# A SwiGLU up projection moved from weights stationary to tokens stationary with its output transposed, and weights split in pieces of 2048 columns

## The chip, the cores and the metric

The kernel runs on one core of a Trainium2 chip. The metric is the time of one execution in microseconds of the device (us), as the median of several runs. The engines that matter are TensorE (PE), which multiplies; VectorE (DVE) and ScalarE (ACT), which do element-wise work; GpSimd (POOL), which does small powers; and SyncE (SP), whose queue starts the transfers from memory.

## The reference

An encoder trunk of two layers (`DEPTH` = 2) in fp32, on 256 tokens of width 1024. Each layer is a half-step FFN, a mixing step of three branches, and another half-step FFN. The change is in the FFNs, and in how weights are made ready in all stages. `D_FF` is 2816. Cut to what matters:

```python
def swiglu(h, w_up, w_down):
    a, b = jnp.split(h @ w_up, 2, axis=-1)
    return (jax.nn.silu(a) * b) @ w_down
...
    for l in range(DEPTH):
        h = rms_norm(x, ffn1_pre_g[l])
        x = x + 0.5 * rms_norm(swiglu(h, ffn1_w_up[l], ffn1_w_down[l]), ffn1_post_g[l])
        h = rms_norm(x, mix_pre_g[l])
        u_pool, q_da, k_da, v_da, q_ca = jnp.split(h @ w_in[l], IN_SPLITS, axis=-1)
        ...
        x = x + rms_norm(merged @ w_out[l], mix_post_g[l])
        h = rms_norm(x, ffn2_pre_g[l])
        x = x + 0.5 * rms_norm(swiglu(h, ffn2_w_up[l], ffn2_w_down[l]), ffn2_post_g[l])
```

Between the two FFNs of a layer (the left-out lines) stand a pooling branch, a differential attention with two softmaxes per head, and a cross attention into 256 normed memory tokens; three gates weigh them.

## The kernel before

**Split weights and products.** Every weight arrives in units of 128 partitions x 2048 columns of fp32 (1 MB), each by one DMA on SP's queue (`load_unit`, L96-102). `next_unit` (L104-120) splits a unit in two tensors of the type fp32r: ACT casts a high part `wh` (L115), DVE subtracts it from the raw unit to get a low part `wl` (L116). The first five units of a stage (`FINE`) are split in four pieces of 512 columns, the others in two of 1024: ACT casts the first piece, DVE subtracts it while ACT casts the second. The raw units have 3 buffers, `wh` and `wl` 5 each. The activations are split in the same way (`split`, L148-150; ACT L149, DVE L150). A product is three matmuls: high x high, high x low, low x high.

**The FFN** (`ffn`, L266 on). The hidden columns go in 11 pairs p of 256 columns (2 x 128 of each half of `w_up`). The tokens are two chunks c of 128. Two forms of the up projection stand in the code:

- p = 0 and 1 use `up(p, c, ws)` (L295-312), called for each token chunk. The 128 tokens (`xhl`, the split and transposed input) are stationary, and 512 weight columns move: 256 for the Silu and 256 for the factor, 8 blocks of 128 rows, 24 matmuls into one PSUM bank `ma` (`form_b2` L232, `mm3`, its matmul is L207). Then ACT takes the Silu of one half (L300), DVE multiplies by the other (L302). The result has tokens on partitions, where `down` needs hidden columns there, so two PE transposes follow (L307, into a bank `mb`) and a split (L149, L150) into `hid[p]`. These are put off: `turn` is put on a list and `flush` issues it behind the matmuls of the next `up` or `up2`, or in the last part of the FFN.
- p = 2 to 10 use `up2(p, u)` (L314-327), called for each 128 hidden columns u. Here the weights are stationary and the tokens move (`form_a2`, L218-226): 512 moving columns (256 tokens high, 256 low, in four pieces of 128 of a tile) with the high weights, and 256 (two pieces) with the low ones, 16 matmuls for each of two banks, `ma` and `mb`. The result has hidden columns on partitions already. ACT copies out the low half of a bank (L323), DVE adds the high one (L324), for both banks; then the Silu (L325), the product (L326) and the split into `hid[p]`.

`down(p)` (L281) multiplies `hid[p]`, stationary, with a unit of `w_down`, 512 columns moving, 24 matmuls (L249). `down(p - 2)` follows `up` of p as long as p is at most 9; the last three p come in `tail` (L256), which goes through the token chunks one after the other, with `flush` between them. In the first FFN of a layer, `ahead()` prepares the memory tokens at p = 4, and PE transposes them (L182, 8 for each chunk, two banks `mb` each) at p = 6.

**The mix** (L406 on). Its input products are L207 as well. The steps of the attention on PE are placed by hand among the big products: `T_DA`, `T_PV`, `T_LN`, `T_CA`, `T_CAV` (L36-41) name after how many matmuls of a stage's count a group of small ones is issued. Before the transposes of `T_DA` (L449) lies a softmax: DVE finds the maximum (L421) and scales it (L423), ACT takes the exponentials (L429), DVE scales and combines (L565, L567, L569, L570). Before those of `T_CA` the scaling is L607 and L612. The copies out of the transposes are ACT's L451.

The order of the instructions within an engine is set by a scheduler when the program is built, and every engine then works strictly in that order: a short step on DVE waits for the long one that stands ahead of it.

Of the kernel before, what the change touches and what calls it, by code (L numbers as in the profile page):

```python
# [13 lines left out]
AF = mybir.ActivationFunctionType  # L14
ALU = mybir.AluOpType
AX = mybir.AxisListType

P = 128
D = 1024
KT = D // P  # L20
S = 256
DEPTH = 2
D_FF = 2816
# [23 lines left out]
def encoder_kernel(ctx, tc, x_d, mem_d, pos_d, w_d, gains_d, cols_d, lamv_d, poolw_d, cst_d, out_d):  # L47
    nc = tc.nc
# [15 lines left out]
    def acc_bank():  # L64
        return accp.tile([P, 512], F32, name="acc")

    def ma_bank():
        return mmp.tile([P, 512], F32, name="ma")

    def mb_bank():  # L70
        return mmp.tile([P, 512], F32, name="mb")

    def t2(shape=(P, 512), dt=F32):
        return s2.tile(list(shape), dt, name="s2")
# [19 lines left out]
    fine = [0]  # L94

    def load_unit(parts=1):  # L96
        raw = rawp.tile([P, 2048], F32, name="raw")
        n = 2048 // parts
        for i in range(parts):
            nc.sync.dma_start(out=raw[:, i * n:(i + 1) * n], in_=w_d[nxt[0]][:, i * n:(i + 1) * n])  # L100
        nxt[0] += 1
        raws.append(raw)

    def next_unit():  # L104
        parts = 4 if fine[0] > 0 else 2
        fine[0] -= 1
        if not raws:
            load_unit()
        raw = raws.pop(0)
        h = wts.tile([P, 2048], F32R, name="wh")  # L110
        l = wts.tile([P, 2048], F32R, name="wl")
        n = 2048 // parts
        for s in range(parts):
            cs = slice(s * n, (s + 1) * n)
            nc.scalar.copy(out=h[:, cs], in_=raw[:, cs])  # L115
            low = nc.vector.tensor_tensor(out=l[:, cs], in0=raw[:, cs], in1=h.bitcast(F32)[:, cs], op=ALU.subtract)  # L116
            if nxt[1] == 0:
                issue_after([low], first_xn[1])
        nxt[1] += 1
        return h, l  # L120
# [27 lines left out]
    def split(ps, h, l):  # L148
        nc.scalar.copy(out=h, in_=ps)  # L149
        nc.vector.tensor_tensor(out=l, in0=ps, in1=h.bitcast(F32), op=ALU.subtract)  # L150
# [60 lines left out]
    def kview(w):  # L211
        return w[0].rearrange("p (k m) -> p k m", k=KT), w[1].rearrange("p (k m) -> p k m", k=KT)
# [2 lines left out]
        wh, wl = kview(w)  # L215
        return mm3(out, [((wh[:, k, ms], wl[:, k, ms]), (xx[0][:, :, k, :], xx[1][:, :, k, :])) for k in range(KT)])

    def form_a2(out, w, ms, xx):  # L218
        wh, wl = kview(w)
        full, low = out, out[:, 0:S]  # L220
        for k in range(KT):
            todo = [(full, wh, xx[2][:, :, k, :]), (low, wl, xx[2][:, 0:2, k, :])]
            if k == KT - 1:
                todo.reverse()
            for o, ww, rhs in todo:
                nc.tensor.matmul(out=o, lhsT=ww[:, k, ms], rhs=rhs, start=(k == 0 and o is full), stop=(k == KT - 1 and o is full))  # L226

    def form_b(out, w, c, xx):
        wh, wl = kview(w)
        return mm3(out, [((xx[0][:, c, k, :], xx[1][:, c, k, :]), (wh[:, k, :], wl[:, k, :])) for k in range(KT)])  # L230
# [38 lines left out]
    def ffn(i, xx, late, g_post, finish, ahead):  # L269
        fine[0] = FINE  # L270
        hid = {}
        acc = [[None, None], [None, None]]

        def hid_pair(p):
            hid[p] = (hids.tile([P, 2, 2, P], F32R, name="hid"), hids.tile([P, 2, 2, P], F32R, name="hid"))
            return hid[p]

        def lhs_of(c, kk, k):
            return hid[kk][0][:, c, k, :], hid[kk][1][:, c, k, :]

        def down(p):  # L281
            w = next_unit()
            if p == 0:
                for c in range(2):
                    acc[c] = [acc_bank(), acc_bank()]
            for c in range(2):
                rows_chunk(c, acc[c], [(w, p)], lhs_of, 0, NPR - 1)

        pending = []

        def flush():
            while pending:
                pending.pop(0)()

        def up(p, c, ws):  # L295
            ps = ma_bank()
            now = form_b2(ps, ws[0], ws[1], c, xx)
            flush()
            sg = t2((P, 2, P))
            nc.scalar.activation(out=sg, in_=ps[:, 0:256].rearrange("p (u m) -> p u m", u=2), func=AF.Silu)  # L300
            hn = t2((P, 2, P))
            nc.vector.tensor_tensor(out=hn, in0=ps[:, 256:512].rearrange("p (u m) -> p u m", u=2), in1=sg, op=ALU.mult)  # L302

            def turn():
                tp = mb_bank()
                for u in range(2):
                    nc.tensor.transpose(out=tp[:, u * P:(u + 1) * P], in_=hn[:, u, :], identity=ident)  # L307
                tv = tp[:, 0:256].rearrange("p (u t) -> p u t", u=2)
                split(tv, hid[p][0][:, c], hid[p][1][:, c])

            pending.append(turn)
            return now

        def up2(p, u):  # L314
            w = next_unit()
            banks = [ma_bank(), mb_bank()]
            for i in range(2):
                form_a2(banks[i], w, slice(i * P, (i + 1) * P), xx)
            flush()
            t = t2()  # L320
            for i in range(2):
                half = t[:, i * S:(i + 1) * S]
                nc.scalar.copy(out=half, in_=banks[i][:, S:2 * S])  # L323
                nc.vector.tensor_tensor(out=half, in0=banks[i][:, 0:S], in1=half, op=ALU.add)  # L324
            nc.scalar.activation(out=t[:, 0:S], in_=t[:, 0:S], func=AF.Silu)  # L325
            nc.vector.tensor_tensor(out=t[:, 0:S], in0=t[:, 0:S], in1=t[:, S:2 * S], op=ALU.mult)  # L326
            split(t[:, 0:S].rearrange("p (c t) -> p c t", c=2), hid[p][0][:, :, u, :], hid[p][1][:, :, u, :])

        ws = [(next_unit(), next_unit()) for _ in range(2)]
        for p in range(2):  # L330
            hid_pair(p)
        done = []
        order = [(0, 0), (0, 1), (1, 0), (1, 1)] if i > 0 else [(0, 0), (1, 0), (0, 1), (1, 1)]
        for c, p in order:
            now = up(p, c, ws[p])
            done += now
            if len(done) == (48 if i > 0 else 24):
                issue_after(late, done[T_UP if i > 0 else T_FIRST])
        for p in range(2, NPR):
            hid_pair(p)  # L340
            for u in range(2):
                up2(p, u)
            if p - 2 <= NPR - 4:
                down(p - 2)
            if p == 4:
                turns = ahead()
            if p == 6:
                for t in turns:
                    t()
        todo = [(next_unit(), p) for p in range(NPR - 3, NPR)]  # L350
        return tail(acc, todo, lhs_of, 0, NPR - 1, g_post, True, finish, flush)
# [427 lines left out]
def _pack(a, np):  # L779
    L = DEPTH  # L780
    units = []

    def cols(w, idx):
        units.append(np.ascontiguousarray(w[:, idx].reshape(KT, P, 256).transpose(1, 0, 2)).reshape(P, 2048))

    def wide(w, idx):
        both = w[:, idx].reshape(2, 4, P, 512).transpose(0, 2, 1, 3)
        units.extend(np.ascontiguousarray(both[i]).reshape(P, 2048) for i in range(2))

    def rows(w, j):  # L790
        units.append(np.ascontiguousarray(w[256 * j:256 * (j + 1)].reshape(2, P, D).transpose(1, 0, 2)).reshape(P, 2048))

    def ffn(up, down):
        for p in range(NPR):
            if p < 2:
                wide(up, np.r_[256 * p:256 * p + 256, D_FF + 256 * p:D_FF + 256 * p + 256])
            else:
                for i in (2 * p, 2 * p + 1):
                    cols(up, np.r_[P * i:P * i + P, D_FF + P * i:D_FF + P * i + P])
            if 0 <= p - 2 <= NPR - 4:  # L800
                rows(down, p - 2)
        for p in range(NPR - 3, NPR):
            rows(down, p)

    for l in range(L):
        ffn(a["ffn1_w_up"][l], a["ffn1_w_down"][l])
        wi = a["w_in"][l]
        for s in (256, 768, 1280):
            wide(wi, slice(s, s + 512))
        for s in (0, 1792):  # L810
            cols(wi, slice(s, s + 256))
        for s in (0, 256):
            cols(a["w_mem_kv"][l], slice(s, s + 256))
        for i in range(6):
            wide(a["w_gate"][l], slice(512 * i, 512 * i + 512))
        br = np.concatenate([a["w_br_pool"][l], a["w_br_da"][l], a["w_br_ca"][l]], axis=0)
        for i in range(2):
            wide(br, slice(512 * i, 512 * i + 512))
        for j in range(4):
            rows(a["w_out"][l], j)  # L820
        ffn(a["ffn2_w_up"][l], a["ffn2_w_down"][l])
    return np.stack(units)
# [38 lines left out]
```

## Time and profile before

| what | value |
|---|---|
| time, median of 3 runs | 1155.15 us (1155.0 to 1155.38) |
| span of the profiled execution | 1154.1 us |
| PE busy | 1141.8 us, 5930 matmuls and transposes |
| DVE, ACT busy | 768.6 us, 634.1 us |
| memory read | 215.80 MB, 188 GB/s over the span |

The profiled execution is one of its own; its page shows the span, which lies about 1 us under the median time, for what lies around it. "Busy" of PE counts a matmul from its start to its modelled end, which lies in the next one's time, so the durations of matmuls (0.39 us) overlap and what one costs in a row is the distance from start to start. On ACT and DVE the durations also overlap a little. A row of the groups has the line, the engine, the operation, the tile written and the tiles read, the shapes, the count, the busy time and the mean of one, then the idle time of the engine ahead of the group and what ended it.

### The profile page before, as it was taken

How to read it: one execution, taken by the hardware profiler on the slowest of the kernel's cores; microseconds unless marked ns; L12 is line 12 of the kernel's file. 1: busy time of each engine (PE TensorE's matmuls, PEld its weight loads, DVE VectorE, ACT ScalarE, POOL GpSimd, SP SyncE). 2: the span in 40 equal slices, each digit the busy share in tenths (PEclk: the TensorE clock that was granted, in tenths of full speed). 3: DMA queues.
4: the chain of work that ended last, by engine and by line, in shares of the span. 5: the costliest groups of instructions: out<-in, count | busy, mean ns of one | idle time of the engine just before them, and what ended most of it. 6: DMA issues, size and time to landing. Idle time of an engine off the chain costs nothing.

```text
span 1154.1 us, 15241 instructions
## 1 busy us (share of the span) xinstructions
PE 1141.8 (99%) x5930; PEld 963.4 (83%) x5930; DVE 768.6 (67%) x1198; ACT 634.1 (55%) x1141; POOL 28.6 (2%) x39
## 2 busy tenths in 40 slices
PE   8999999999999999999999999999999999999997
PEld 5888888898888888888888888888978888888886
DVE  5768665665767876665586766675677678666653
ACT  5657554644665555555465655556455646555551
POOL 0000000000000100000000000010000001000000
PEclk8999999999999999999999999999999999999999
DMA  8865554564444575555456665535535544755530
GB/s 298 299 236 213 183 183 146 183 219 146 164 172 162 194 271 191 183 182 189 176 191 228 223 216 180 185 141 192 209 120 194 201 165 166 248 190 182 183 110 36
DMA packets 34055, 217.82 MB, mean 189 GB/s; under 512 B 4032, under 2 KB 4288, under 8 KB 9664
## 3 DMA queue, kind: packets, MB, share of 16 engines
q1 hardware_dynamic: 33984, 216.86, 53.0%
q8 instruction: 46, 0.75, 0.3%
q14 instruction: 25, 0.20, 0.0%
HBM read 215.80 MB, written 1.05 MB: 188 GB/s over the span
## 4 chain that ended last, share of the span: by engine, by line
PE 98%; DMA 1%; ACT 0%; SPq 0%; issue 0%; DVE 0%; DVEq 0%; POOLq 0%; ACTq 0%
PE ma L207 30%; PE acc L249 25%; PE mb L226 18%; PE ma L226 18%; PE mb L207 2%; PE mb L182 1%; PE acc L207 1%; PE acc L560 1%; DMA raw<-in_w 1%; PE mb L449 1%; PE acc L577 1%; PE acc L618 1%; PE acc L603 1%; PE mb L307 0%; PE mb L691 0%; PE mb L507 0%
## 5 line engine op out<-in xcount | busy, mean ns | idle before, releaser
L116 DVE TENSOR_TENSOR wl<-raw,wh 128x1024 fp32r<-128x1024 f32 (+1 forms) x444 | 460.2, 1077 | 140.2 <-ACT wh L115 125.9
L115 ACT CAST wh<-raw 128x1024 fp32r<-128x1024 f32 (+1 forms) x444 | 392.1, 935 | 169.8 <-issue 112.4
L207 PE MATMUL ma<-wh,xhl 128*128 128x512 f32 (+1 forms) x928 | 290.5, 390 | 1.9 <-ACT xhl L149 1.9
L249 PE MATMUL acc<-wh,hid 128*128 128x512 f32 x704 | 223.8, 390 | 0.0
L226 PE MATMUL ma<-xhl,wh 128*128 128x512 f32 x576 | 209.9, 399 | 0.0
L226 PE MATMUL mb<-xhl,wh 128*128 128x512 f32 x576 | 209.3, 398 | 0.0
L207 PEld LDWEIGHTS ma<-wh,xhl 128*128 128x128 f32 x928 | 172.8, 190 | 37.5 <-ACT xhl L149 2.2
L207 PE MATMUL ma<-wl,xhl 128*128 128x512 f32 (+1 forms) x464 | 180.2, 388 | 0.0
L249 PEld LDWEIGHTS acc<-wh,hid 128*128 128x128 f32 x704 | 132.2, 188 | 26.1
L226 PE MATMUL ma<-xhl,wl 128*128 128x256 f32 x576 | 150.1, 281 | 0.0
L226 PE MATMUL mb<-xhl,wl 128*128 128x256 f32 x576 | 150.1, 281 | 0.0
L249 PE MATMUL acc<-wl,hid 128*128 128x512 f32 x352 | 137.1, 389 | 0.0
L226 PEld LDWEIGHTS ma<-xhl,wh 128*128 128x128 f32 x576 | 108.2, 188 | 20.9
L226 PEld LDWEIGHTS mb<-xhl,wh 128*128 128x128 f32 x576 | 108.7, 189 | 19.2
L324 DVE TENSOR_TENSOR s<-mb,s 128x256 f32<-128x256 f32 x72 | 30.6, 425 | 130.2 <-ACT s L323 130.1
L226 PEld LDWEIGHTS mb<-xhl,wl 128*128 128x128 f32 x576 | 109.0, 189 | 6.6
L226 PEld LDWEIGHTS ma<-xhl,wl 128*128 128x128 f32 x576 | 108.8, 189 | 5.9
L207 PEld LDWEIGHTS ma<-wl,xhl 128*128 128x128 f32 x464 | 88.2, 190 | 17.3 <-issue 1.3
L249 PEld LDWEIGHTS acc<-wl,hid 128*128 128x128 f32 x352 | 66.2, 188 | 13.9
L325 ACT ACTIVATE s<-s 128x256 f32<-128x256 f32 x72 | 30.1, 418 | 69.5 <-DVE s L324 69.5
L323 ACT COPY s<-mb 128x256 f32<-128x256 f32 x72 | 26.8, 372 | 74.3 <-PE mb L226 74.3
L134 POOL TENSOR_TENSOR sm<-sm,mhalf 128x1 f32<-128x1 f32 (+1 forms) x32 | 27.9, 871 | 1119.8 <-DVE sm L143 855.2
(153 smaller groups left out, 991.3 us busy)
## 6 DMA issues: line engine op xcount, KB each, us to landing
raw<-in_w SPq DMA_DIRECT2D x190, 1024.0 KB, 4.9
gain<-in_gains SPq DMA_DIRECT2D x20, 512.0 KB, 5.2
raw<-in_w SPq DMA_DIRECT2D x4, 512.0 KB, 8.3
hid<-in_mem SPq DMA_DIRECT2D x8, 256.0 KB, 6.0
x<-in_x SPq DMA_DIRECT2D x4, 256.0 KB, 6.3
out<-x SPq DMA_DIRECT2D x4, 256.0 KB, 2.1
cst<-in_cst SPq DMA_DIRECT2D x1, 304.0 KB, 5.3
pw<-in_poolw SPq DMA_DIRECT2D x2, 128.0 KB, 4.0
```

The source lines that it names most:

```text
L115: nc.scalar.copy(out=h[:, cs], in_=raw[:, cs])
L116: low = nc.vector.tensor_tensor(out=l[:, cs], in0=raw[:, cs], in1=h.bitcast(F32)[:, cs], op=ALU.subtract)
L134: nc.gpsimd.tensor_tensor(out=r, in0=v, in1=mhalf[:, :n], op=ALU.pow)
L182: tps.append(nc.tensor.transpose(out=ps[:, k * P:(k + 1) * P], in_=xn[:, i * P:(i + 1) * P], identity=ident))
L207: done.append(nc.tensor.matmul(out=out, lhsT=lhsT, rhs=rhs, start=(i == 0), stop=(i == n - 1)))
L226: nc.tensor.matmul(out=o, lhsT=ww[:, k, ms], rhs=rhs, start=(k == 0 and o is full), stop=(k == KT - 1 and o is full))
L249: done.append(nc.tensor.matmul(out=banks[b], lhsT=a, rhs=ww[:, k, fs], start=(kk == first and k == 0 and i == 0), stop=(kk == last and k = ...
L323: nc.scalar.copy(out=half, in_=banks[i][:, S:2 * S])
L324: nc.vector.tensor_tensor(out=half, in0=banks[i][:, 0:S], in1=half, op=ALU.add)
L325: nc.scalar.activation(out=t[:, 0:S], in_=t[:, 0:S], func=AF.Silu)
L449: ins.append(nc.tensor.transpose(out=tp[:, i * P:(i + 1) * P], in_=a[:, hh, kt * P:(kt + 1) * P], identity=ident))
L560: nc.tensor.matmul(out=banks[m][:, hh * S:(hh + 1) * S], lhsT=qT[rs, c, 2 * hp + hh, :], rhs=kT[rs, :, 2 * hp + hh, :], start=True, stop=True)
```

## The change

All pairs p use the form of p = 0 and 1. The two units of a pair are now packed as p = 0 and 1 had them (512 wide: 256 columns of each half of `w_up`, 4 of the 8 row blocks in each unit), `up(p, c, w2)` is called for both chunks, and `form_a2` and `up2` go. The number and size of the units stay. Apart from the first five units of a stage, a unit is split whole: one cast of 2048 columns and one subtraction. In the new code, lines up to about L313 stand 10 lower (L307 becomes L297, L249 L239, L300 L290, L302 L292) and those behind 24 lower (L421 becomes L397, L423 L399, L449 L425, L570 L546, L612 L588).

```diff
     def next_unit():
-        parts = 4 if fine[0] > 0 else 2
+        parts = 4 if fine[0] > 0 else 1
         fine[0] -= 1
...
-    def form_a2(out, w, ms, xx):
-        wh, wl = kview(w)
-        full, low = out, out[:, 0:S]
-        for k in range(KT):
-            todo = [(full, wh, xx[2][:, :, k, :]), (low, wl, xx[2][:, 0:2, k, :])]
-            if k == KT - 1:
-                todo.reverse()
-            for o, ww, rhs in todo:
-                nc.tensor.matmul(out=o, lhsT=ww[:, k, ms], rhs=rhs, start=(k == 0 and o is full), stop=(k == KT - 1 and o is full))
...
-        def up2(p, u):
-            w = next_unit()
-            banks = [ma_bank(), mb_bank()]
-            for i in range(2):
-                form_a2(banks[i], w, slice(i * P, (i + 1) * P), xx)
-            flush()
-            t = t2()
-            for i in range(2):
-                half = t[:, i * S:(i + 1) * S]
-                nc.scalar.copy(out=half, in_=banks[i][:, S:2 * S])
-                nc.vector.tensor_tensor(out=half, in0=banks[i][:, 0:S], in1=half, op=ALU.add)
-            nc.scalar.activation(out=t[:, 0:S], in_=t[:, 0:S], func=AF.Silu)
-            nc.vector.tensor_tensor(out=t[:, 0:S], in0=t[:, 0:S], in1=t[:, S:2 * S], op=ALU.mult)
-            split(t[:, 0:S].rearrange("p (c t) -> p c t", c=2), hid[p][0][:, :, u, :], hid[p][1][:, :, u, :])
...
         for p in range(2, NPR):
             hid_pair(p)
-            for u in range(2):
-                up2(p, u)
+            w2 = (next_unit(), next_unit())
+            for c in range(2):
+                up(p, c, w2)
             if p - 2 <= NPR - 4:
                 down(p - 2)
...
         for p in range(NPR):
-            if p < 2:
-                wide(up, np.r_[256 * p:256 * p + 256, D_FF + 256 * p:D_FF + 256 * p + 256])
-            else:
-                for i in (2 * p, 2 * p + 1):
-                    cols(up, np.r_[P * i:P * i + P, D_FF + P * i:D_FF + P * i + P])
+            wide(up, np.r_[256 * p:256 * p + 256, D_FF + 256 * p:D_FF + 256 * p + 256])
```

The first place is on PE, in the first FFN, p = 8. Before, its second half ends with the bank `mb_1378`, and `down` (L249, into `acc_498`) follows:

```order
L226 MATMUL mb_1378<-xhl_110,wl_1372 128x256
L226 MATMUL mb_1378<-xhl_110,wh_1371 128x512
L226 MATMUL mb_1378<-xhl_110,wl_1372 128x256 x2
L226 MATMUL mb_1378<-xhl_110,wh_1371 128x512
L249 MATMUL acc_498<-wh_1422,hid_1016 128x512
L249 MATMUL acc_498<-wl_1423,hid_1016 128x512
```

In the new order a group of two transposes (L297) stands behind each `up`, one ahead of the second `up` (bank `ma_1217`) and one ahead of `down` (L239); each turns the product of the `up` before the last one issued:

```order
L207 MATMUL ma_1183<-wh_1179,xhl_110 128x512
L297 MATMUL mb_1208<-ident_95,s2_1137 128x128 x2
L207 MATMUL ma_1217<-wh_1173,xhl_110 128x512
...
L207 MATMUL ma_1217<-wh_1179,xhl_110 128x512
L297 MATMUL mb_1242<-ident_95,s2_1215 128x128 x2
L239 MATMUL acc_471<-wh_1253,hid_917 128x512
```

So PE loses the L226 rows of 512 and 256 columns and gains rows of L207 and the two groups. The second place is on DVE in the mix of the first layer, ahead of the transposes `T_DA[0]`. Before, half a unit (`wl_2780`) stands between the maximum (L421) and its scaling (L423), and the other half behind it:

```order
L116 TENSOR_TENSOR wl_2772<-raw_2769,wh_2771 128x1024 x2
L421 TENSOR_REDUCE sm_2395<-acc_2388 128x2
L421 TENSOR_REDUCE sm_2395<-acc_2389 128x2
L116 TENSOR_TENSOR wl_2780<-raw_2777,wh_2779 128x1024
L423 TENSOR_SCALAR sm_2398<-sm_2395 128x4
L116 TENSOR_TENSOR wl_2780<-raw_2777,wh_2779 128x1024
```

In the new order the whole unit (`wl_2546`) stands between them:

```order
L116 TENSOR_TENSOR wl_2540<-raw_2537,wh_2539 128x2048
L397 TENSOR_REDUCE sm_2167<-acc_2160 128x2
L397 TENSOR_REDUCE sm_2167<-acc_2161 128x2
L116 TENSOR_TENSOR wl_2546<-raw_2543,wh_2545 128x2048
L399 TENSOR_SCALAR sm_2170<-sm_2167 128x4
```

The half that stood behind the scaling stands ahead of it now. The third place is DVE again, ahead of `T_CA[1]`, before:

```order
L421 TENSOR_REDUCE sm_2637<-acc_2630 128x2
L421 TENSOR_REDUCE sm_2637<-acc_2631 128x2
L116 TENSOR_TENSOR wl_3141<-raw_3138,wh_3140 128x1024
L423 TENSOR_SCALAR sm_2640<-sm_2637 128x4
L116 TENSOR_TENSOR wl_3141<-raw_3138,wh_3140 128x1024
```

and now:

```order
L397 TENSOR_REDUCE sm_2409<-acc_2402 128x2
L397 TENSOR_REDUCE sm_2409<-acc_2403 128x2
L116 TENSOR_TENSOR wl_2889<-raw_2886,wh_2888 128x2048
L399 TENSOR_SCALAR sm_2412<-sm_2409 128x4
L632 TENSOR_TENSOR hid_2776<-ma_2751,gain_2737 128x512
```

Here too the second half has moved ahead of the scaling. In both mixes the order is the same.

## The prediction

> **What bounds the kernel now.** I read the page first, then the waits of the matrix engine, then its timeline at the places the diff touches. From the page, in the order of its parts: the engines and the chain that ended last.
>
> ```profile
> PE 1141.8 (99%) x5930; PEld 963.4 (83%) x5930; DVE 768.6 (67%) x1198; ACT 634.1 (55%) x1141; POOL 28.6 (2%) x39
> PE 98%; DMA 1%; ACT 0%; SPq 0%; issue 0%; DVE 0%; DVEq 0%; POOLq 0%; ACTq 0%
> ```
>
> The waits of the matrix engine, with total, count and longest:
>
> ```profile
> PE mb L182 <- DVE s L172: 2.2, 1, 2.2
> PE ma L207 <- ACT xhl L149: 1.9, 1, 1.9
> PE mb L725 <- DVE up L530: 1.2, 1, 1.2
> ```
>
> PE is on the chain for 98% of the span and waits 5.3 us in three places. So the time is the sum of PE's start-to-start times, and only two things can move it: what PE executes, and any new wait of PE. ACT at 55% and DVE at 67% have time to spare; work taken from them gains nothing by itself, but work put into longer pieces can make PE wait where a short step stands behind a long piece.
>
> **The change on PE.** The hidden pairs p = 2 to 10 of each of the four FFNs (36 in all) go from the old form to the form that p = 0 and 1 already use, so both forms stand in the trace of before. Two periods of the old form, one `down` between them (start, duration, engine, line; the rows left out are matmuls of these lines):
>
> ```profile
> 56.11 0.39 PE L226 MATMUL ma<-xhl,wh 128*128 128x512 f32 x1
> ...
> 67.39 0.40 PE L249 MATMUL acc<-wh,hid 128*128 128x512 f32 x1
> ...
> 72.83 0.39 PE L226 MATMUL ma<-xhl,wh 128*128 128x512 f32 x1
> ```
>
> One pair in the old form, four banks of 16 matmuls, takes 67.39 - 56.11 = 11.28 us, 5.64 to the half. `down`'s 24 matmuls, 512 columns each and with a moving operand in one run, take 72.83 - 67.39 = 5.44, which is 0.227 each. The new form has 48 matmuls of that sort to a pair: 48 x 0.227 = 10.88. That saves 0.40 per pair, because the old moving operand, in four (or two) pieces of 128 columns, streams more slowly than its width says: a 512 and a 256 together take 11.28/32 = 0.3525, where one and a half of the 0.227 would be 0.340.
>
> Against it stand two groups of two transposes per pair, which the old form did not need. The same groups as they run now, behind p = 0 and 1 of the first FFN:
>
> ```profile
> 27.51 0.38 PE L307 MATMUL mb<-ident,s 128*128 128x128 f32 x2
> 27.65 0.48 PE L207 MATMUL ma<-wh,xhl 128*128 128x512 f32 x1
> 27.96 0.40 PE L207 MATMUL ma<-wl,xhl 128*128 128x512 f32 x1
> ...
> 33.22 0.38 PE L307 MATMUL mb<-ident,s 128*128 128x128 f32 x2
> 33.36 0.48 PE L207 MATMUL ma<-wh,xhl 128*128 128x512 f32 x1
> ...
> 38.94 0.38 PE L307 MATMUL mb<-ident,s 128*128 128x128 f32 x2
> 39.07 0.48 PE L226 MATMUL ma<-xhl,wh 128*128 128x512 f32 x1
> ...
> 44.80 0.38 PE L307 MATMUL mb<-ident,s 128*128 128x128 f32 x2
> ```
>
> A group takes 33.36 - 33.22 = 0.14 itself, and has a wake: the first matmul behind it takes 27.96 - 27.65 = 0.31 instead of 0.227. From group to group, with 24 matmuls of `up` between, it is 33.22 - 27.51 = 5.71 and 38.94 - 33.22 = 5.72; less the 5.44 of 24 undisturbed matmuls, 0.275 per group. With one old half behind the group it is 44.80 - 39.07 = 5.73 against 5.64, a wake of only 0.09, so 0.23 with the group. In the new order one group of a pair is followed by `up` (the 0.275 row) and one by `down`, which no row shows; I take 0.25 for that one, halfway.
>
> Per pair: 0.275 + 0.25 - 0.40 = +0.125; for 36 pairs **+4.5 us**. The ends: both groups at 0.23 give 36 x 0.06 = +2.2; both at 0.275 give 36 x 0.15 = +5.4. Nothing hides these: PE has no idle time there to put them into. The transposes wait for the Silu and the product of the `up` before. These have the 5.4 us of the next `up`, or 10.9 with a `down` between, and need about 1 us, plus one long cast and one long subtraction at worst (below: 1.9 and 2.2); so I expect no wait there. What falls away on ACT and DVE (copies and adds of the old form) is off the path: nothing.
>
> The page "TensorE: Matmul & The Clock Gate" of the Trainium skill, section "Back-to-back issue gap", gives N/2.4 + 2.5 ns between lone matmuls, 215.8 for 512 columns, 109.2 for 256 and 55.8 for 128. By it, an estimate, the old pair is 10.40 us and the new one 10.58, and the term would be +6.5 instead of +4.5. The trace's 0.227 for 512 columns is above its figure, and neither the slower four-piece operand nor the wake is in it, so the rows decide.
>
> **The change on ACT and DVE: one piece of 2048 instead of two of 1024.** The price of a piece (busy, mean ns of one):
>
> ```profile
> L115 ACT CAST wh<-raw 128x1024 fp32r<-128x1024 f32 x324 | 325.7, 1051 | 163.0 <-issue 112.4 <-PE ma L207 34.8 <-PE acc L249 5.8
> L115 ACT CAST wh<-raw 128x512 fp32r<-128x512 f32 x120 | 66.6, 621 | 6.8 <-DMA raw<-in_w 4.9 <-PE acc L249 1.8
> L116 DVE TENSOR_TENSOR wl<-raw,wh 128x1024 fp32r<-128x1024 f32 x324 | 383.9, 1222 | 133.1 <-ACT wh L115 118.8 <-PE ma L207 8.9 <-issue 0.8
> L116 DVE TENSOR_TENSOR wl<-raw,wh 128x512 fp32r<-128x512 f32 x120 | 76.5, 685 | 7.1 <-ACT wh L115 7.0
> ```
>
> By these slopes a cast of 2048 takes 1051 + 2 x 430 = 1911 ns and a subtraction 1222 + 2 x 537 = 2296. Successive instructions overlap by about 0.09 (below, 264.39 to 265.52 is 1.13 for 1222 ns), so a subtraction holds DVE for 2.21 instead of 1.13. In the FFNs units are cast about one pair ahead, behind 10.9 us of PE's matmuls, so this costs nothing; without that cover it would be 0.9 + 1.1 at each pair. In the mix, transposes stand at fixed places in PE's order, right behind softmax chains of ACT and DVE. Two places have neither slack nor a clear way.
>
> First T_DA[0]. DVE, then PE, then ACT before it:
>
> ```profile
> 264.39 1.22 DVE L116 TENSOR_TENSOR wl<-raw,wh 128x1024 fp32r<-128x1024 f32 x1
> 265.52 0.17 DVE L423 TENSOR_SCALAR sm<-sm 128x4 f32<-128x4 f32 x1
> ...
> 270.37 0.88 DVE L570 SCALAR_TENSOR_TENSOR s<-s,sm,s 128x256 f32<-128x256 f32 x2
> ```
>
> ```profile
> 271.42 0.60 PE L449 MATMUL mb<-ident,s 128*128 128x128 f32 x4
> ```
>
> ```profile
> 262.61 2.00 ACT L115 CAST wh<-raw 128x1024 fp32r<-128x1024 f32 x2
> ```
>
> The chain L423, exponentials, L570 ends at 271.25 and PE comes at 271.42: slack 0.17. In the new order the subtraction ahead of L423 is a whole one. It starts when its cast ends, 262.61 + 1.91 = 264.52 and a hand-over (about 0.05), and lets L423 run at 266.78 instead of 265.52: 1.26 late. PE waits 1.26 - 0.17 = **1.1 us**.
>
> Second T_CA[1]:
>
> ```profile
> 326.95 0.16 DVE L423 TENSOR_SCALAR sm<-sm 128x4 f32<-128x4 f32 x1
> ...
> 329.41 1.14 DVE L612 TENSOR_SCALAR s<-s,sm 128x256 f32<-128x256 f32 x4
> ```
>
> ```profile
> 329.91 0.63 PE L449 MATMUL mb<-ident,s 128*128 128x128 f32 x4
> ```
>
> Here L612 ends at 330.55, after PE has begun with the first of its four parts: no slack. Ahead of L423 now stands a half subtraction, in the new order a whole one: it comes 2.21 - 1.13 = 1.08 later, and PE waits **1.1 us**. Behind the waiting transposes PE's whole queue stands, so both waits go into the time in full.
>
> The other placed steps I followed through both orders: their chains either have no unit in them or come out level. The nearest is T_PV[2], whose copy L451 stands behind three half casts now and behind two whole ones then; that uses up about the slack it has, and I allow 0.15 for it and the like. Per mix 2.35, two mixes **+4.7 us** (bounds: 0, if DVE runs the pieces otherwise, and 2 x 4.5, if two more steps of each mix lose 1.08).
>
> Last the memory transposes in the first FFN of each layer: the second eight need the banks that the first eight used.
>
> ```profile
> 123.00 1.04 PE L182 MATMUL mb<-ident,s 128*128 128x128 f32 x8
> ...
> 126.21 1.25 PE L182 MATMUL mb<-ident,s 128*128 128x128 f32 x8
> ```
>
> ```profile
> 123.24 1.05 ACT L115 CAST wh<-raw 128x1024 fp32r<-128x1024 f32 x1 [2.92 <-issue]
> ```
>
> ```profile
> 125.47 1.28 DVE L150 TENSOR_TENSOR xhl<-mb,xhl 128x512 fp32r<-128x512 f32 x2
> ```
>
> In the new order a whole cast and a whole subtraction stand ahead of L150: 123.24 + 1.91 + 0.05 + 2.21 = 127.4, and the first bank is free at 128.1. PE's second eight now come behind 18 matmuls of `up` instead of 13 of the old form: 123.00 + 0.79 + 18 x 0.227 + 0.13 = 128.0. So 0.1 in each layer, **+0.2 us** (bounds 0 and 2 x 1.1, if the matmuls are placed otherwise).
>
> A sentence of the page "Perfetto Trace Analysis", section "Optimizing Scalar/DVE Operations", speaks against this part of the change: "If Scalar/Vector aren't saturated, but are causing bubbles on other engines, breaking up instructions may allow work to be completed sooner." The rows above bear it out in before, where L423 gets in between two halves; its own result would be the sum with the +4.7, and without it the sum is 4.7 smaller.
>
> **Sum.** The profiled execution has a span of 1154.1; the runs have a median of 1155.15, so 1.05 lies around the span. 1154.1 + 4.5 + 4.7 + 0.2 = 1163.5, and with 1.05: **1164.5 us**. The bounds of the costs: with the two waits of each mix there, 1155.15 + 2.2 + 4.4 = 1161.7 and 1155.15 + 5.4 + 5.2 + 2.2 = 1168.
>
> **Rivals.** *The wake is not there in a steady pipeline* (the end on the other side). The groups in the trace run where the FFN begins and pieces are fine; if a group costs its 0.14 alone, 36 x (0.28 - 0.40) = -4.3, and the mix's +4.7 brings it to 1155.5, no change; without those waits too it would be 1150.9. It decides at 0.20 per group. For it speaks that wakes differ (0.09 to 0.135). Against it: all three groups shown come to 0.23 or more.
>
> *The mix's waits do not come*, since a chain there is shorter than I followed it or PE arrives later: 1155.15 + 4.5 = 1159.7, with the 0.2 of the memory 1159.9 (1157.4 to 1160.6). For it: ACT and DVE have more idle time in sum. Against it: both places have slack under 0.2 and the whole piece is ahead of L423 in the order.
>
> *More placed steps are hit.* Each mix has 14, and several have little slack; two more in each at 1.08 give +4.3, 1168.8; five, 1175. It decides where a step's slack is under 1.08 and a whole piece starts just ahead of it. Against it: only the two showed this in the order.
>
> *The change does little*, because the two PE terms and the split cancel otherwise: 1155.
>
> **How the numbers follow.** Forecast case (1161.7 to 1168) 0.66; waits of the mix absent 0.12; more steps hit 0.12; no wake 0.06 (half of it faster, half no change); cancelling 0.04. 0.2% is 2.3 us, about what a measurement here can tell from no change. Faster: half of the no-wake case and a little of cancelling, 0.05. Same: the other half, most of cancelling, the bottom of the second rival, 0.07. Slower: 0.88. The range 1158 to 1169 leaves out the first and last rivals, the bottom of the second and the upper half of the third, some 0.18.
>
> **What would show it.** In the changed profile the time from one `up` group of transposes to the next with one `up` between should be 5.71, and a pair with its `down` 5.72 + 5.69 + 5.44 = 16.85 where it was 16.72. The waits of PE should have four new entries of about 1.1 us at the transposes of the softmax, behind the products L546 and L588. If the period is 16.6 or less, the wake was wrong; if those entries are missing, the chain in the mix was; if PE waits for L292 in the FFNs, the spare time I gave the Silu was.

## The result and the profile after

The changed kernel takes 1161.14 us (median of 4 runs, 1160.17 to 1162.2) beside 1155.27 of the kernel before on the same chips: ratio 1.0051, 95% interval 1.0039 to 1.0063, 5.9 us slower. The prediction said slower, 1164.5, range 1158 to 1169. The direction and the FFN's part were right; the part of the mix was nearly four times too large. The time lies in the range, but below the bounds of the forecast case (1161.7 to 1168). The answers to the rows of before, first the page's engines and chain:

```profile
PE 1147.3 (99%) x5498; PEld 945.2 (82%) x5498; DVE 700.5 (60%) x892; ACT 564.2 (49%) x834; POOL 27.6 (2%) x39
PE 97%; DMA 1%; DVE 1%; ACT 0%; issue 0%; SPq 0%; POOL 0%; DVEq 0%; POOLq 0%; ACTq 0%
```

ACT and DVE each lost about 70 us of work, as `up2`'s copies and adds went and the splits became fewer, and the time still rose: PE is still the sum. The page's span is 1159.2, 5.1 above before's 1154.1 (that execution of before lies 0.4 to 0.6 above the median span of the same kernel in the experiments). The waits of PE:

```profile
PE ma L207 <- ACT xhl L149: 2.1, 1, 2.1
PE mb L182 <- DVE s L172: 1.3, 1, 1.3
PE mb L701 <- DVE up L506: 1.2, 1, 1.2
PE ma L207 <- DVE wl L116: 0.2, 1, 0.2
```

The four waits of 1.1 us that the prediction named are not among them. Where the 5.1 us are, the transposes L182 tell, with which a stage hands its result to the next; the first of them marks the end of a stage (PE; before, then after; the three rows of a kernel enclose the mix of the first layer and the FFN behind it):

```profile
200.60 0.27 PE L182 MATMUL mb<-ident,s 128*128 128x128 f32 x1
...
390.25 0.27 PE L182 MATMUL mb<-ident,s 128*128 128x128 f32 x1
...
578.91 0.27 PE L182 MATMUL mb<-ident,s 128*128 128x128 f32 x1
```

```profile
200.62 0.27 PE L182 MATMUL mb<-ident,s 128*128 128x128 f32 x1
...
390.89 0.27 PE L182 MATMUL mb<-ident,s 128*128 128x128 f32 x1
...
580.95 0.27 PE L182 MATMUL mb<-ident,s 128*128 128x128 f32 x1
```

The mix grew from 189.65 to 190.27, by 0.62; the FFN behind it from 188.66 to 190.06, by 1.40. By the same marks the second mix grew by 0.60, the FFN ahead of it by 0.98 and the last one by 1.44. The first FFN ends only 0.02 later, because its opening was shorter in this execution: PE's first wait at L182 is 1.3 here and 2.2 before. So two mixes are 1.2, and the FFNs hold the rest. A period of the new form (PE):

```profile
60.35 0.38 PE L297 MATMUL mb<-ident,s 128*128 128x128 f32 x2
60.49 0.48 PE L207 MATMUL ma<-wh,xhl 128*128 128x512 f32 x1
...
66.05 0.38 PE L297 MATMUL mb<-ident,s 128*128 128x128 f32 x2
66.18 0.48 PE L239 MATMUL acc<-wh,hid 128*128 128x512 f32 x1
...
71.74 0.39 PE L207 MATMUL ma<-wh,xhl 128*128 128x512 f32 x1
...
77.18 0.38 PE L297 MATMUL mb<-ident,s 128*128 128x128 f32 x2
```

From 60.35 to 77.18 is 16.83 for a pair and its `down`, where it was 16.72: +0.11, and 16.85 was forecast. A group costs 66.05 - 60.35 - 5.44 = 0.26 in front of `up` and 71.74 - 66.05 - 5.44 = 0.25 in front of `down`. This price is not the same in every FFN. In the two FFNs behind a mix the distances are 5.71 and 11.15 throughout, 16.86 in sum, so a group costs 0.02 more there; 22 groups make 0.44 of the 1.40. The run with pieces of 1024 in the mix alone (below) has 5.69 in the same FFNs, with the same code, and there they lose 0.95 and 0.98. What makes the 0.02 stays open.

Now the two places in the mix. DVE ahead of T_DA[0], before (two rows that the prediction had overlooked), then after, and the transposes on PE after:

```profile
268.89 0.69 DVE L656 TENSOR_TENSOR hid<-ma,gain 128x512 f32<-128x512 f32 x1 [2.09 <-PE ma L207]
269.50 0.17 DVE L565 RECIPROCAL sm<-sm 128x4 f32<-128x4 f32 x1
```

```profile
264.56 2.29 DVE L116 TENSOR_TENSOR wl<-raw,wh 128x2048 fp32r<-128x2048 f32 x1
266.77 0.16 DVE L399 TENSOR_SCALAR sm<-sm 128x4 f32<-128x4 f32 x1
268.91 0.69 DVE L632 TENSOR_TENSOR hid<-ma,gain 128x512 f32<-128x512 f32 x1 [1.98 <-PE ma L207]
270.27 0.18 DVE L541 RECIPROCAL sm<-sm 128x4 f32<-128x4 f32 x1 [0.67 <-ACT s L405]
```

```profile
271.68 0.83 PE L425 MATMUL mb<-ident,s 128*128 128x128 f32 x4
```

The scaling comes at 266.77, within 0.01 of the forecast 266.78, 1.25 later than before. But the reciprocal comes only 0.77 later (270.27 against 269.50): before, it stood behind the gate's addition L656, which itself had to wait for PE until 268.89. So half a microsecond of the delay fell where the chain had been waiting anyway. PE's transposes start 0.26 later and take 0.23 longer (0.83 against 0.60 for the four rows): 0.49 in place of the forecast 1.1.

T_CA[1] after, DVE and PE:

```profile
326.34 2.28 DVE L116 TENSOR_TENSOR wl<-raw,wh 128x2048 fp32r<-128x2048 f32 x1
328.54 0.16 DVE L399 TENSOR_SCALAR sm<-sm 128x4 f32<-128x4 f32 x1
```

```profile
331.72 1.15 PE L425 MATMUL mb<-ident,s 128*128 128x128 f32 x8
```

The scaling comes at 328.54 (326.95 before), the transposes 331.72 - 329.91 = 1.81 later than before, and the profile names no wait of PE there: the new order has 49 of the big products (matmuls of L207) between T_CA[0] and T_CA[1], where before had 44. Of the two runs below that make one half of the change each, the one with whole pieces has 49 as well and the one with halves 44, so this change of order goes with the split. The whole mix is only 0.62 longer. So the theory to test was: the FFN's loss is what PE executes; the whole pieces cost 0.5 us at T_DA[0] and about 0.1 at T_PV[2] in each mix; and the delay at T_CA[1] is real, but paid with products that PE had to do anyway.

### The profile page after: what moved, and what is told of

Same layout as the page of the kernel before. It is cut to its first block, busy times and chain, and to the rows that moved or that the text cites. A ratio compares the mean times of both kernels' runs of the same rounds, so it can differ in the third digit from the quotient of the medians.

```text
span 1159.2 us, 13895 instructions
## 1 busy us (share of the span) xinstructions
PE 1147.3 (99%) x5498; PEld 945.2 (82%) x5498; DVE 700.5 (60%) x892; ACT 564.2 (49%) x834; POOL 27.6 (2%) x39
## 4 chain that ended last, share of the span: by engine, by line
PE 97%; DMA 1%; DVE 1%; ACT 0%; issue 0%; SPq 0%; POOL 0%; DVEq 0%; POOLq 0%; ACTq 0%
PE ma L207 63%; PE acc L239 25%; PE mb L207 2%; PE mb L297 2%; PE mb L182 1%; PE acc L207 1%; PE acc L536 1%; PE mb L425 1%; DMA raw<-in_w 1%; PE acc L553 1%; PE acc L594 1%; PE acc L579 1%; PE mb L667 0%; PE mb L483 0%; ACT s L405 0%; PE mb L615 0%
## 5 line engine op out<-in xcount | busy, mean ns | idle before, releaser
L207 PE MATMUL ma<-wh,xhl 128*128 128x512 f32 (+1 forms) x2080 | 661.2, 392 | 2.1 <-ACT xhl L149 2.1
L116 DVE TENSOR_TENSOR wl<-raw,wh 128x2048 fp32r<-128x2048 f32 (+1 forms) x282 | 446.2, 1607 | 285.9 <-ACT wh L115 277.1
L115 ACT CAST wh<-raw 128x2048 fp32r<-128x2048 f32 (+1 forms) x282 | 375.9, 1365 | 262.1 <-PE acc L239 102.5
L207 PEld LDWEIGHTS ma<-wh,xhl 128*128 128x128 f32 x2080 | 388.4, 188 | 81.6 <-ACT xhl L149 2.3
L207 PE MATMUL ma<-wl,xhl 128*128 128x512 f32 (+1 forms) x1040 | 404.2, 389 | 0.2 <-DVE wl L116 0.2
L239 PE MATMUL acc<-wh,hid 128*128 128x512 f32 x704 | 228.5, 396 | 0.0
L207 PEld LDWEIGHTS ma<-wl,xhl 128*128 128x128 f32 x1040 | 196.0, 188 | 39.2 <-issue 1.3
L239 PEld LDWEIGHTS acc<-wh,hid 128*128 128x128 f32 x704 | 132.2, 188 | 26.7
L239 PE MATMUL acc<-wl,hid 128*128 128x512 f32 x352 | 137.3, 390 | 0.0
L290 ACT ACTIVATE s<-ma 128x256 f32<-128x256 f32 x88 | 33.8, 384 | 161.5 <-PE ma L207 161.5
L239 PEld LDWEIGHTS acc<-wl,hid 128*128 128x128 f32 x352 | 66.3, 188 | 12.7
L292 DVE TENSOR_TENSOR s<-ma,s 128x256 f32<-128x256 f32 x88 | 36.8, 418 | 57.0 <-ACT s L290 57.0
L239 PE MATMUL acc<-wh,xhl 128*128 128x512 f32 x128 | 41.0, 394 | 0.0
L150 DVE TENSOR_TENSOR hid<-mb,hid 128x256 fp32r<-128x256 f32 x88 | 36.5, 415 | 0.0
L207 PE MATMUL ma<-xhl,wh 128*128 128x256 f32 x192 | 34.6, 283 | 0.0
L297 PEld LDWEIGHTS mb<-ident,s 128*128 128x128 f32 x176 | 24.4, 139 | 11.4
L297 PE MATMUL mb<-ident,s 128*128 128x128 f32 x176 | 33.5, 272 | 0.0
```

Of the source, the lines that this page charges most:

```text
L207: done.append(nc.tensor.matmul(out=out, lhsT=lhsT, rhs=rhs, start=(i == 0), stop=(i == n - 1)))
L239: done.append(nc.tensor.matmul(out=banks[b], lhsT=a, rhs=ww[:, k, fs], start=(kk == first and k == 0 and i == 0), stop=(kk == last and k = ...
```

## The experiments

**The two halves of the change apart.** The changed kernel with the old split:

```diff
-        parts = 4 if fine[0] > 0 else 1
+        parts = 4 if fine[0] > 0 else 2
```

> The changed kernel with the split of before: pieces of 1024 columns beside the new up projection. Theory (the time comes from what PE executes; the whole pieces cost only some 0.6 us in each mix): 1155.3 + 4.4 = 1159.7 us, some 1.2 under the changed kernel; a pair with its down again takes 16.83 us; the transposes T_DA[0] wait no longer. Rival (the whole pieces are the larger part of the loss): 1157 or less.

Measured 1159.8 us (1159.44 to 1160.6), ratio to before 1.0038, interval 1.0024 to 1.0052. The five runs of this kernel lie 2.1 us above their own spans, those of before 1.8; by the median spans, 1157.7 and 1153.7, the up projection costs 4.0. The transposes T_DA[0] no longer wait for each other (0.60 for the four, as before):

```profile
271.43 0.60 PE L425 MATMUL mb<-ident,s 128*128 128x128 f32 x4
```

And the reverse, the kernel before with whole pieces:

```diff
-        parts = 4 if fine[0] > 0 else 2
+        parts = 4 if fine[0] > 0 else 1
```

> The kernel before with whole pieces of 2048 columns and nothing else changed. Theory: the mix loses 0.6 us a layer, at T_DA[0] (about 0.5) and at T_PV[2] (0.1), and T_CA[1] loses nothing since it is issued about five matmuls later; 1155.3 + 1.2 = 1156.5 us. The prediction's own account (1.1 at each of T_DA[0] and T_CA[1]): 1160. Rival (the whole pieces also cost in the FFNs): 1158 or more, with waits of PE in the FFNs.

Measured 1157.02 us (1156.62 to 1157.6) beside 1155.44: ratio 1.0015, interval 1.0006 to 1.0024. T_DA[0] is held here as in the changed kernel (0.83 for the four):

```profile
271.26 0.83 PE L449 MATMUL mb<-ident,s 128*128 128x128 f32 x4
```

The halves add up, within intervals of 1 us and more: 4.4 for the up projection and 1.6 for the split are 6.0, and 5.9 was measured for both. The rival that gives the whole pieces the larger part is out, and the prediction's 4.7 for the split too.

**The split in the mix alone.** Pieces of 1024 in the mix, whole ones in the FFNs (the variable is set to 1 where an FFN begins):

```diff
-        parts = 4 if fine[0] > 0 else 1
+        parts = 4 if fine[0] > 0 else coarse[0]
...
     def mix(l, xx, late, mm, finish):
...
+        coarse[0] = 2
         fine[0] = FINE
```

> The changed kernel with pieces of 1024 in the mix alone; in the FFNs the units past the fifth are split whole. Theory (the whole pieces cost only in the mix): 1159.8 us, as with halves everywhere. Rival (they cost in the FFNs too): between 1160.3 and 1161.

Measured 1160.03 us (1159.17 to 1160.49), ratio 1.0042, interval 1.0029 to 1.0054. That is near the 1159.8 of halves everywhere. The difference between the two theories, at most 1 us, is about the width of the intervals; the time agrees with whole pieces being free in the FFNs, but does not settle a few tenths. The marks of the stages (the first transposes to the next stage, as above) do. The two mixes take 189.62 and 189.61 here and 189.64 and 189.62 with halves everywhere, but 190.27 and 190.26 in the changed kernel and 190.30 and 190.32 in the kernel before with whole pieces: 0.63 to 0.7 for each mix. The FFN behind the first mix takes 189.61 here with whole pieces, and 190.07 with halves everywhere, where its groups have the higher price; so no cost of the pieces shows in it.

**Was T_CA[1] really delayed?** In the changed kernel the transposes T_CA[1] were kept ahead of the product that they had preceded before:

```diff
         for at, ins in placed:
             issue_after(ins, fill[at])
+            if at == T_CA[1]:
+                issue_after([fill[456]], ins[-1])
```

> The changed kernel with the transposes T_CA[1] of both mixes kept ahead of the product that they preceded before (within one matmul), some six products earlier than where the changed order has them; nothing else is held. Theory (the whole piece does delay the softmax by 1.1 us there, and the order makes up for it by putting other products in front): PE waits about 1.3 us in each mix, 1161 + 2.6 = 1163.6. Rival (the softmax is not delayed, or the delay is hidden elsewhere): no change from 1161.

Measured 1163.71 us (1162.81 to 1164.15), ratio 1.0072, interval 1.006 to 1.0085; 2.6 over the changed kernel. The waits of PE, and the place in the first mix:

```profile
PE mb L425 <- DVE s L588: 2.7, 2, 1.3
```

```profile
332.21 1.15 PE L425 MATMUL mb<-ident,s 128*128 128x128 f32 x8 [1.35 <-DVE s L588]
```

This is the wait that the prediction worked out, two of them, up to 1.35 us each. The transposes have 552 of the mix's big products ahead of them here and 553 before; without the 0.227 of this one product the wait is 1.12, and 1.1 was forecast. The softmax is delayed; what saved the changed kernel at this place is the order alone.

**What a group of transposes costs.** The prediction split a group's 0.25 into 0.137 of its own and a wake in the matmul behind it. If a wake is paid once per group, fewer and larger groups save it. The changed kernel with the four transposes of a pair (p = 2 to 9) in one group, behind the next pair's first `up`:

```diff
+            held.append((c, hn))
+            if 2 <= p < NPR - 1 and c == 0:
+                return now
+            todo = list(held)
+            held.clear()
...
             def turn():
                 tp = mb_bank()
-                for u in range(2):
-                    nc.tensor.transpose(out=tp[:, u * P:(u + 1) * P], in_=hn[:, u, :], identity=ident)
+                for j, (cc, hh) in enumerate(todo):
+                    for u in range(2):
+                        i = 2 * j + u
+                        nc.tensor.transpose(out=tp[:, i * P:(i + 1) * P], in_=hh[:, u, :], identity=ident)
```

> The changed kernel with the transposes of both token chunks of p = 2 to 9 issued together, four in one group instead of two groups of two; 32 groups fewer, no transpose fewer. Rival one (the prediction's account: a group costs 0.137 itself, and a fixed wake of 0.113 in what follows): 32 x 0.113 = 3.6 us less than the changed kernel, 1157.5. Rival two (there is no fixed wake; each transpose costs 0.109 us, and what shows in the matmul behind it is the last transpose's own time, with 0.03 us per group on top): 32 x 0.03 = 1.0 us less, 1160.1.

Measured 1160.56 us (1159.42 to 1161.2), ratio 1.0044, interval 1.0031 to 1.0056. A group of four:

```profile
61.71 0.60 PE L308 MATMUL mb<-ident,s 128*128 128x128 f32 x4
62.07 0.47 PE L207 MATMUL ma<-wh,xhl 128*128 128x512 f32 x1
62.38 0.39 PE L207 MATMUL ma<-wl,xhl 128*128 128x512 f32 x1
```

Four take 0.36, 0.22 more than two, and the first matmul behind them again 0.31. By the time alone a gain of 0.6 us cannot be told from none, but 3.6 is excluded. So it is by the trace: from group to group, a pair and its `down` take 16.78 to 16.81, and one wake of 0.113 less would have made 16.72 of the 16.83. Then the same with each transpose issued twice:

```diff
                     nc.tensor.transpose(out=tp[:, u * P:(u + 1) * P], in_=hn[:, u, :], identity=ident)
+                    if p >= 2:
+                        nc.tensor.transpose(out=tp[:, 256 + u * P:256 + (u + 1) * P], in_=hn[:, u, :], identity=ident)
```

> The changed kernel with each transpose of p = 2 to 10 issued twice, the second into an unused part of the bank: 72 groups of four instead of two. Theory (a transpose costs 0.109 us from start to start, and what shows behind the group is the last one's own time): 72 x 0.218 = 15.7 us over the changed kernel, 1176.8. Rival (0.068 each and a fixed wake of 0.113 per group): 72 x 0.137 = 9.8, 1171.

Measured 1178.79 us (1177.87 to 1179.4), ratio 1.0204, interval 1.019 to 1.0218; 17.6 over the changed kernel. The group, one row for each transpose:

```profile
60.94 0.27 PE L297 MATMUL mb<-ident,s 128*128 128x128 f32 x1
61.05 0.27 PE L299 MATMUL mb<-ident,s 128*128 128x128 f32 x1
61.16 0.27 PE L297 MATMUL mb<-ident,s 128*128 128x128 f32 x1
61.27 0.27 PE L299 MATMUL mb<-ident,s 128*128 128x128 f32 x1
61.30 0.48 PE L207 MATMUL ma<-wh,xhl 128*128 128x512 f32 x1
```

Each starts 0.11 behind the one ahead, the last is followed after 0.03, and the missing 0.08 shows in the matmul behind (as in the group of four above, 0.31 to its successor instead of 0.227). So a transpose costs 0.109, the last one's share is booked on its neighbour, and of the wake some 0.03 per group is left (0.25 less 0.218). 72 x 0.218 = 15.7 of the 17.6; 0.9 more is one new wait, where the transposes once come too early:

```profile
PE mb L297 <- DVE s L292: 0.9, 1, 0.9
```

About 1 us of the 17.6 stays unaccounted for. In the profiles most of it lies in the first FFN, whose opening differs from run to run: PE's first wait at L182 is 2.7 us here, 1.3 in the changed kernel and 0.2 in the last run below.

**Why the old form streams more slowly than its columns say.** The prediction put the 0.40 us of a pair down to the four pieces of 128 columns in the moving operand. The kernel before with the tokens' tile laid out so that the operand is one run:

```diff
-        t = xts.tile([P, 2, 2, KT, P], F32R, name="xhl")
-        return t[:, 0], t[:, 1], t.rearrange("p s c k t -> p (s c) k t")
+        t = xts.tile([P, KT, 2, 2, P], F32R, name="xhl")
+        return t[:, :, 0].rearrange("p k c t -> p c k t"), t[:, :, 1].rearrange("p k c t -> p c k t"), t.rearrange("p k s c t -> p (s c) k t")
```

> The kernel before with another layout of the split tokens: for each block of 128 rows the high and the low part of both chunks stand side by side, so that the moving operand of the old up projection is one run of 512 (or 256) columns instead of four (or two) pieces of 128. Theory (the old form loses 0.39 us a pair because of the pieces): a pair takes 32 x 0.340 = 10.88 us instead of 11.28, and the time is 1155.3 - 36 x 0.39 = 1141 us. Rival (it loses them because a 256-column matmul cannot hide its weight load): a pair stays at 11.28 and the time at 1155.

Measured 1154.74 us (1154.12 to 1156.24), ratio 0.9997, interval 0.9988 to 1.0005: no change. A pair:

```profile
54.73 0.39 PE L226 MATMUL ma<-xhl,wh 128*128 128x512 f32 x1
...
66.00 0.40 PE L249 MATMUL acc<-wh,hid 128*128 128x512 f32 x1
```

66.00 - 54.73 = 11.27, as before. The pieces are not the cause. The next suspect was the turns of wide and narrow matmuls. The kernel before with the widths of a bank apart:

```diff
         for k in range(KT):
-            todo = [(full, wh, xx[2][:, :, k, :]), (low, wl, xx[2][:, 0:2, k, :])]
-            if k == KT - 1:
-                todo.reverse()
+        todo = [(k, full, wh, xx[2][:, :, k, :]) for k in range(KT - 1)]
+        todo += [(k, low, wl, xx[2][:, 0:2, k, :]) for k in range(KT)]
+        todo += [(KT - 1, full, wh, xx[2][:, :, KT - 1, :])]
```

> The kernel before; in each bank of the old up projection seven of the matmuls of 512 columns come first, then the eight of 256, then the last of 512, instead of taking turns. With the layout of the tokens out of the question, the theory is that the turns cost: a 512 behind a 256 takes 0.236 us instead of 0.227, since its weights come late. Then 512s in a row take 0.227 and 256s in a row 0.120 as in the mix: a bank takes 2.78 instead of 2.82, a pair 11.10, and the time is 36 x 0.17 = 6 us less, 1149. Rival (a 512 of this operand takes 0.236 in any order): no gain or, with the 256s at 0.120, 1156.

Measured 1151.84 us (1151.25 to 1152.59), ratio 0.9972, interval 0.996 to 0.9983: 3.4 us faster than before, where 6 was expected. A pair, and the eight narrow matmuls inside it:

```profile
55.67 0.39 PE L225 MATMUL ma<-xhl,wh 128*128 128x512 f32 x1
...
57.26 1.11 PE L225 MATMUL ma<-xhl,wl 128*128 128x256 f32 x8
58.21 0.40 PE L225 MATMUL ma<-xhl,wh 128*128 128x512 f32 x1
...
66.83 0.40 PE L248 MATMUL acc<-wh,hid 128*128 128x512 f32 x1
```

The eight take 58.21 - 57.26 = 0.95, 0.119 each. The pair takes 66.83 - 55.67 = 11.16 instead of 11.28. So 0.12 of the 0.40 hangs on the order of the widths, and the rest is still there. Sorted over a whole unit:

```diff
+        todo = [(k, i, 0) for i in range(2) for k in range(KT - 1)]
+        todo += [(k, i, 1) for i in range(2) for k in range(KT)]
+        todo += [(KT - 1, i, 0) for i in range(2)]
```

> The kernel before with the matmuls of a whole unit of the old up projection sorted by width over both banks: 14 of 512 columns, then 16 of 256, then the last two of 512; two changes of width in a pair of units instead of four. In the kernel sorted by bank the 256s ran at 0.120 and the first five 512s behind them were 0.027 us long in sum, and a pair took 11.15. Theory (that lag is paid once per change of width): 2 x 0.027 less per pair, 36 x 0.054 = 1.9 us less than the 1151.8 of that kernel, 1149.9. Rival (each 256 adds to the lag, and it is paid in full): no change, 1151.8.

Measured 1151.24 us (1149.0 to 1151.51), ratio 0.9965, interval 0.9953 to 0.9978. A pair:

```profile
53.57 0.39 PE L226 MATMUL ma<-xhl,wh 128*128 128x512 f32 x1
...
64.69 0.39 PE L249 MATMUL acc<-wh,hid 128*128 128x512 f32 x1
```

It takes 11.12, 0.04 less than sorted by bank where the theory asked for 0.054 and the rival for nothing; by the time it cannot be told from the kernel sorted by bank. Of the 0.40, 0.16 has gone with the order; 32 x (0.119 - 0.227/2) = 0.18 is what narrow matmuls cost above half a wide one even in a row; 0.06 stays open. This version has the lowest median of those run, 4.1 us below before and 9.9 below the changed kernel.

## Why the prediction was right, and where it was wrong

**The number.** The direction rests on PE's share, and that was worked out. That the range held rests on its width: it also takes in 1159.7, the rival without waits in the mix, to which the prediction gave 0.12 and which is nearer to 1161.14 than the forecast 1164.5. What came lies between the two, since of three terms for the mix one failed, one was halved and one held.

**PE's share, +4.5 forecast: right, for partly wrong reasons.** With halves everywhere the new up projection alone costs 4.4 us by the time and 4.0 by the spans. The period came out at 16.83 and 16.86, by the FFN, and 16.85 was forecast. The price of a group was right, since it was taken from a whole distance in the trace (5.71 less 5.44); the 0.25 in front of `down` was a guess that no row showed, and it came out. The explanation was not right: there is no wake that a larger group would save, but for some 0.03, and there are two transposes of 0.109. And the 0.40 saved per pair was a right difference of two measured distances, while its reason, the four-piece operand, fell: laid out in one run the operand streams no faster.

**The waits at T_CA[1], 2 x 1.1 forecast, none found.** The step that failed is "PE's whole queue stands" behind the waiting transposes: the prediction held PE's order fixed at the place it has in the trace of before. The delay is real (1.35 us of wait when the place is held), but the order of the changed kernel has five more products in front of the transposes. The marks by which the mix is placed are lower bounds (`issue_after`), and the order is made anew for every program. The prediction takes DVE's order at this place from the new program, and PE's from the trace of before.

**The wait at T_DA[0], 1.1 forecast, 0.49 found.** The step that failed is the sum of the chain from L423 to L570 as if every row of it moved by the same 1.26. The scaling and the exponentials did, the reciprocal by 0.77, because before it had been held by an addition that waits for PE. A delay at a chain's head arrives at its end less the waits inside the chain.

**T_PV[2], 0.15 allowed, 0.11 found.** ACT and PE after:

```profile
291.89 3.72 ACT L115 CAST wh<-raw 128x2048 fp32r<-128x2048 f32 x2
295.49 0.60 ACT L427 COPY s<-mb 128x512 f32<-128x512 f32 x1
```

```profile
296.14 1.16 PE L553 MATMUL acc<-wl,s 128*128 128x128 f32 x8
297.23 0.49 PE L536 MATMUL acc<-wh 64*128 64x256 f32 x2
```

The copy stands behind the two whole casts and ends at 296.09; the eight products that need it start at 296.14 and take 1.09, where before they took 0.98. It is a place with no slack left, as the prediction had it. With the 0.49 of T_DA[0] this makes 0.60 of the mix's 0.62.

**The memory transposes, +0.2 forecast, 0.17 found.** PE after:

```profile
122.22 1.04 PE L182 MATMUL mb<-ident,s 128*128 128x128 f32 x8
127.31 0.66 PE L182 MATMUL mb<-ident,s 128*128 128x128 f32 x4
```

Here the prediction had PE's new order, and the 18 matmuls that it counted stand between the two groups. By its sum the second group could start at 122.22 + 0.79 + 18 x 0.227 + 0.13 = 127.23; it starts at 127.31. From the group of `up` ahead of it to the one behind it is 13.12 and 13.11 in the two layers, and 13.04 and 13.02 with halves everywhere. The waits are too short to stand in the list of PE's waits.

**The FFNs' cover.** The profile after names no wait for the Silu's product in an FFN, and apart from the memory transposes no cost of whole pieces shows there, as the stages of the run that has halves in the mix alone bear out.

**The page "TensorE: Matmul & The Clock Gate" of the Trainium skill, section "Back-to-back issue gap".** By its gap for lone matmuls the FFN's term would have been +6.5, an estimate; measured was 4.4. The 215.8 ns of that gap for 512 columns stand against 0.227 us here, and its 55.8 for 128 columns against 0.109 for a transpose of 128 fp32 columns; the measurement decides.

**The page "Perfetto Trace Analysis" of the Trainium skill, section "Optimizing Scalar/DVE Operations".** Its advice to break instructions up where ACT or DVE hold others back agrees in direction with the 1.2 to 1.6 us that the whole pieces cost here, though DVE's busy time fell by 68 us in all.

## What to carry to other kernels

Where one engine is busy for 99% of the span, price a change by start-to-start distances of whole groups on that engine, not by durations of single rows: a cost can be booked on the neighbour. Before a new wait is counted, compare the new order of the waiting engine too, since a scheduler may put other work in front of it, and follow the delayed chain row by row, since a wait inside it takes up part of the delay. A cause that merely fits a difference, like the pieces of the operand here, is worth a run of its own: the run that refuted it led to an order of matmuls that beats both kernels.

## What the runs showed of the hardware

A 512-column matmul in this kernel takes 0.227 us from start to start, and a run of 256-column ones 0.119 each, more than half of that. In turns, a 512 and a 256 take 11.28/32 = 0.3525 together; by those two prices it would be 0.346. Sorting them by width makes a pair of units 0.12 to 0.16 us shorter without any other change. That the weights of the matmul after a narrow one come late would fit this, as the loads take 0.188 us each and a narrow matmul covers less of it; that is only argued, no run measured it by itself. The trace of before does not place the extra time there: it has 0.236 us from the start of a wide matmul to the narrow one behind it, and 0.117 from the narrow one to the wide one behind it (means over the old form). But as the transposes show, a cost can be booked on a neighbour, so the cause stays open.
